# Splitting the merged rows where they are made, keeping the parts in DRAM for W_mix_out, and putting A11 and A12 together on TensorE

## The chip, the cores and the metric

The kernel runs on one core of one Trainium2 chip. The metric is the device time of one execution in microseconds (us). Three runs of the kernel before gave 2270.32, 2273.77 and 2274.34 us, so its median is 2273.77 us. The profile was taken of one further execution.

## The reference, cut to what matters

One layer works on 1024 tokens of width 1024. It is a half-step feed-forward layer, a token-mixing layer and a second half-step feed-forward layer, each between two RMS norms. All matrices are float32. The change lies at the end of the token mixing and at the start of the second feed-forward layer:

```python
def _token_mixing(u, ...):
    ...
    y_ret = (jax.nn.silu(rg) * y) @ w_ret_out
    y_na = _neighborhood_attention(...) @ w_na_out
    merged = jax.nn.sigmoid(g_ret) * y_ret + jax.nn.sigmoid(g_na) * y_na
    return merged @ w_out                      # W_mix_out, 1024 x 1024

    m = _token_mixing(_rms_norm(x, mix_pre_norm[l]), ...)
    x = x + _rms_norm(m, mix_post_norm[l])
    h = _swiglu(_rms_norm(x, ffn2_pre_norm[l]), ffn2_w_in[l], ffn2_w_out[l])
    x = x + 0.5 * _rms_norm(h, ffn2_post_norm[l])
```

## The kernel before, in words

**Float32 products out of three.** Every operand of a product is split into a high part in the type float32r (a cast on ScalarE, L60) and a low part, the rest (a subtraction on VectorE, L61); `Core.split` does both. `mm3` then multiplies high by high, high by low and low by high into one PSUM bank (L87, L88, L89). A product of two 128 x 128 and 128 x 512 blocks is therefore three matmuls, and each 128 x 512 operand costs one ScalarE and one VectorE instruction. `load_w` loads one 512 KB row block of a weight (issued by SyncE into a tile `wraw`, of which there are four) and splits it into two pieces `wh`, `wl`. There are nine places for each of `wh` and `wl`; a piece keeps its place until the last matmul that reads it.

**W_ret_out (L1295 to L1316).** The product is made transposed, one block of 128 features (a *row*) at a time, in groups of rows 0 to 2, 3 to 5, 6 and 7. A row has two banks of 512 tokens; six banks serve the products, so row 3 takes the banks of row 0. In the first group the loop over the eight blocks of the contraction is outside, so that all three rows end together; later rows come one after the other. VectorE reads a row's banks, multiplies them by the retention gate (L1314) and adds the other branch `z` (L1315); the merged row `m` then goes to DRAM (GpSimd issues that store, L67).

**W_mix_out (`out_proj`, L158).** Tokens are the rows of this product. Its groups are token tiles 0 to 2, 3 to 5, 6 and 7 (128 tokens each), and each group runs over all eight blocks k of the contraction. So each row block of W_mix_out and each merged row is fetched again in every group: for every k, `load_w` loads and splits W_mix_out's row block, and `lhs` in `stream` (L678) loads the merged row's columns of these tokens into `graw` and splits them into `gh`, `gl`. In the last three k of a group the loop over tokens is outside, so the tiles of a group end one after the other. Behind each tile comes `Ep`: squares on ScalarE (L219), the norm's factor on GpSimd (`rstd`, L97), scaling and residual on VectorE (L226, L228), a store of the new x issued by GpSimd (L67), squares and `rstd` again, and the second norm (L117). Some matmuls later TensorE transposes the tile (`flip`, L126) and `Winograd.put` files it.

**Winograd factors (`put`, L258).** The second feed-forward layer's first product is done with seven half-size products. For tokens 0 to 511 `put` splits the transposed tile into A11 and A12. For tokens 512 to 1023 it makes A22 and the four sums S1 to S4; S3 and S4 need A11 and A12 again, which are there only as parts, so VectorE subtracts from the high part (L275, L286) and adds the low part (L276, L287).

**Order.** `tc.tile_pool` hands out the buffers, and a scheduler fixes each engine's order when the program is built, ahead of the run. Each engine then works strictly in that order and waits at an instruction for the semaphores it names. Loads that SyncE issues are told by semaphores DMAHW0 to 7, transfers that GpSimd issues by DMASW0 to 7.

**Behind it (`Pairs.lead`, L346).** Twelve products with A11 and A12, "leads", run ahead of the second feed-forward layer and cover the last tiles' norms. Six results wait in PSUM or in the freed `gh`, `gl`, `graw` tiles (`save`).

## Time and profile before

| | |
|---|---|
| median of 3 runs | 2273.77 us |
| the profiled execution | 2273.08 us |
| its span, first to last instruction | 2271.3 us |
| TensorE matmul busy | 2211.0 us, 97% |
| VectorE busy | 1699.6 us, 75% |
| ScalarE busy | 1004.9 us, 44% |
| GpSimd busy | 577.1 us, 25% |
| mean granted TensorE clock | 0.993 |
| DMA | 424.72 MB, mean 187 GB/s |

A row of the profile names the line of the kernel, the engine, the operation and the tiles (out<-in). L60 and L61 are the two halves of a split wherever it is called from, so these rows are told apart by their tiles: `wl<-wraw,wh` belongs to a weight, `gl<-graw,gh` to the streamed rows. Times count from the first instruction. W_ret_out runs from about 1428 to 1516 us, W_mix_out's three groups from there to about 1624 us, and the leads until 1659 us. "POOL" is GpSimd, "SPq" the queue of SyncE. A DMA issued by GpSimd shows as a POOL instruction for the time of its issue; the transfer itself is told by its time to landing.

### The profile page before, as it was taken

What the parts mean: (1) busy time and instruction counts of PE and PEld (TensorE: products, weight loads), DVE (VectorE), ACT (ScalarE), POOL (GpSimd) and SP (SyncE); (2) the same over time, 40 slices, a digit from 0 to 9 for tenths busy, and PEclk for the clock granted to TensorE, in tenths of its full rate; (3) what the DMA queues carried; (4) which work ended last, traced back from release to release, by engine and by line L of the source; (5) the groups of instructions that cost most, each with busy time, mean ns of one, the idle gap of its engine ahead of it and who ended that gap; (6) DMA issues with size and microseconds to landing.
All of it is one profiled execution on the core that took longest, in us unless ns stands there. A gap on an engine that the chain in (4) does not pass through costs nothing.

```text
span 2271.3 us, 30229 instructions
## 1 busy us (share of the span) xinstructions
PE 2211.0 (97%) x10288; PEld 1837.1 (81%) x10288; DVE 1699.6 (75%) x2952; ACT 1004.9 (44%) x2117; POOL 577.1 (25%) x741
## 2 busy tenths in 40 slices
...
GB/s 192 105 170 184 186 183 186 165 271 199 236 176 144 149 194 111 135 196 245 206 163 170 163 218 228 296 211 213 177 114 188 195 189 176 185 139 237 198 234 151
DMA packets 162459, 424.72 MB, mean 187 GB/s; under 512 B 19776, under 2 KB 47552, under 8 KB 162240
## 3 DMA queue, kind: packets, MB, share of 16 engines
...
q14 instruction: 74, 0.61, 0.1%
...
## 4 chain that ended last, share of the span: by engine, by line
PE 42%; issue 7%; DVE 4%; DMA 3%; ACT 2%; POOL 1%; SPq 0%; POOLq 0%; DVEq 0%; ACTq 0%
PE ps L87 13%; PE ps L89 13%; PE ps L88 13%; DMA wraw<-in_dram 1%; PE pt L88 1%; PE pt L87 1%; PE pt L89 1%; DVE wl L61 1%; POOL rstd L97 1%; DMA vraw<-rv 0%; ACT wh L60 0%; DVE x L538 0%; DMA sn<-ev 0%; DVE tmp L117 0%; DMA vraw<-nvg 0%
## 5 line engine op out<-in xcount | busy, mean ns | idle before, releaser
L61 DVE TENSOR_TENSOR wl<-wraw,wh 128x512 fp32r<-128x512 f32 x662 | 479.8, 748 | 88.2 <-ACT wh L60 86.1
L60 ACT CAST wh<-wraw 128x512 fp32r<-128x512 f32 x670 | 390.6, 618 | 244.8 <-PE ps L88 71.0
L87 PE MATMUL ps<-wh,gh 128*128 128x512 f32 x612 | 239.7, 395 | 6.9 <-ACT gh L60 6.1
L88 PE MATMUL ps<-wl,gh 128*128 128x512 f32 x612 | 240.6, 394 | 0.7 <-DVE wl L61 0.7
L89 PE MATMUL ps<-wh,gl 128*128 128x512 f32 x612 | 235.2, 395 | 2.0 <-DVE gl L61 2.0
L61 DVE TENSOR_TENSOR gl<-graw,gh 128x512 fp32r<-128x512 f32 (+2 forms) x178 | 130.4, 736 | 141.0 <-ACT gh L60 138.1
L60 ACT CAST gh<-graw 128x512 fp32r<-128x512 f32 (+2 forms) x178 | 106.5, 601 | 197.8 <-PE ps L88 83.0
L87 PEld LDWEIGHTS ps<-wh,gh 128*128 128x128 f32 x612 | 116.3, 190 | 33.9 <-ACT gh L60 7.8
L89 PEld LDWEIGHTS ps<-wh,gl 128*128 128x128 f32 x612 | 116.1, 191 | 28.3 <-DVE gl L61 4.5
L528 POOL TENSOR_TENSOR q<-q,gain 128x512 f32<-128x512 f32 x30 | 52.8, 1779 | 335.7 <-ACT junk L527 124.0
L88 PEld LDWEIGHTS ps<-wl,gh 128*128 128x128 f32 x612 | 116.3, 190 | 25.2 <-DVE wl L61 1.5
L60 ACT CAST wh<-t 128x512 fp32r<-128x512 f32 x58 | 36.1, 622 | 214.9 <-DVE t L386 214.9
L87 PE MATMUL ps<-a11h,wh 128*128 128x512 f32 x280 | 110.6, 395 | 1.5 <-ACT wh L60 1.5
L87 PE MATMUL ps<-a12h,wh 128*128 128x512 f32 x280 | 110.8, 396 | 0.7 <-ACT wh L60 0.6
L87 PE MATMUL ps<-a22h,wh 128*128 128x512 f32 x280 | 109.8, 392 | 0.0
L89 PE MATMUL ps<-a22h,wl 128*128 128x512 f32 x280 | 109.1, 390 | 0.5 <-DVE wl L61 0.5
L89 PE MATMUL ps<-a12h,wl 128*128 128x512 f32 x280 | 109.6, 391 | 0.0
L88 PE MATMUL ps<-a11l,wh 128*128 128x512 f32 x280 | 109.6, 391 | 0.0
L89 PE MATMUL ps<-a11h,wl 128*128 128x512 f32 x280 | 109.6, 391 | 0.0
L88 PE MATMUL ps<-a12l,wh 128*128 128x512 f32 x280 | 109.4, 391 | 0.0
L88 PE MATMUL ps<-a22l,wh 128*128 128x512 f32 x280 | 109.1, 390 | 0.0
L97 POOL TENSOR_TENSOR rstd<-ss,mhalf 128x1 f32<-128x1 f32 x80 | 59.4, 745 | 184.6 <-DVE ss L221 74.4
...
## 6 DMA issues: line engine op xcount, KB each, us to landing
wraw<-in_dram SPq DMA_DIRECT2D x247, 512.0 KB, 4.4
lead<-in_dram POOLq DMA_DIRECT2D x44, 256.0 KB, 3.8
g0s<-cmb POOLq DMA_DIRECT2D x44, 256.0 KB, 3.0
graw<-g0s SPq DMA_DIRECT2D x44, 256.0 KB, 2.7
wq<-in_dram POOLq DMA_DIRECT2D x44, 256.0 KB, 4.0
g1s<-cmb POOLq DMA_DIRECT2D x44, 256.0 KB, 3.6
graw<-g1s SPq DMA_DIRECT2D x44, 256.0 KB, 2.7
...
```

The source lines that it names most:

```text
L60: nc.scalar.copy(h, src)
L61: (eng or nc.vector).tensor_tensor(l, src, hf, ALU.subtract)
L87: mm(ps, a[0], b[0], start=start, stop=False, skip_group_check=more)
L88: mm(ps, a[0], b[1], start=False, stop=False, skip_group_check=more)
L89: mm(ps, a[1], b[0], start=False, stop=stop, skip_group_check=more)
L97: self.nc.gpsimd.tensor_tensor(r[:, :n], ms, self.mhalf[:, :n], ALU.pow)
L528: (eng or c.nc.gpsimd).tensor_tensor(h if out is None else out, h, self.post[:, b * 512:(b + 1) * 512], ALU.mult)
```

## The change

Three things are done.

**1. Parts instead of rows.** `m` is split right after L1315 of the old kernel, in the W_ret_out loop, into tiles `mh` and `ml` (one buffer each), and both parts are stored to DRAM arrays (`mparts`), where one float32 row was stored. `stream` loads `gh` and `gl` from there, with two DMAs issued by GpSimd, where it loaded `graw` with one of SyncE's and split it. `graw` is gone; `gh` and `gl` have four buffers each instead of three, and the leads' six saved results are cut from these eight tiles.

**2. W_mix_out's blocks.** In the same loop, behind each row i, `load_w` loads and splits row block i of W_mix_out and four stores put its parts into DRAM (`wparts`). In W_mix_out itself the first two groups load and split as before (16 calls); the third group, tokens 768 to 1023, loads the parts: four DMAs of 256 KB issued by GpSimd for each k, no split.

**3. A11, A12.** With an identity matrix in float32r, TensorE adds the two parts of A11 (A12) into a PSUM bank of the tag `pt` (`less`), and VectorE does one subtraction from there instead of a subtraction and an addition. This is used in this stage alone (`whole` is called only for it).

In numbers of instructions, by the code: in the W_ret_out stage 16 more splits for `m`, 16 for W_mix_out, 8 more loads of 512 KB, 40 more stores (48 for 8). In the W_mix_out stage 24 splits fewer for the streamed rows and 16 fewer for the weights, 24 loads of SyncE replaced by 48 of GpSimd, 8 loads of 512 KB replaced by 32 of 256 KB, 8 VectorE additions fewer and 16 matmuls more.

```diff
@@ -242,7 +242,7 @@
     def __init__(self, c, pools, tmp, bufs, spill=None):
-        self.c, self.tmp, self.spill = c, tmp, spill
+        self.c, self.tmp, self.spill, self.ident = c, tmp, spill, None
         self.pools, self.bufs, self.ops = dict(zip(self.NAMES, (pools[i] for i in (0, 0, 1, 2, 2, 2, 2)))), bufs, {}
...
@@ -253,6 +253,23 @@
         return [q[:, :, ts] for q in self.op(n)]
+
+    def whole(self, pool):
+
+        self.ident = pool.tile([P, P], F32R, tag="identr", name="identr", bufs=1)
+        self.c.nc.scalar.copy(self.ident, self.c.ident)
+
+    def less(self, out, n, ts, b):
+
+        nc, (h, l) = self.c.nc, self.part(n, ts)
+        if self.ident is None:
+            nc.vector.tensor_tensor(out, h.bitcast(F32), b, ALU.subtract)
+            nc.vector.tensor_tensor(out, out, l.bitcast(F32), ALU.add)
+            return
+        bank = self.c.bank("pt", 2).rearrange("p (k t) -> p k t", k=4)
+        for j, p in enumerate((h, l)):
+            nc.tensor.matmul(bank, self.ident, p, start=j == 0, stop=j == 1)
+        nc.vector.tensor_tensor(out, bank, b, ALU.subtract)
     def put(self, t, g, pt):
...
@@ -264,16 +281,12 @@
             return self.tmp.tile([P, 4, P], F32, tag="cmb", name="cmb", bufs=4)
-        h1, l1 = [q.bitcast(F32) for q in self.part("a11", ts)]
-        h2, l2 = [q.bitcast(F32) for q in self.part("a12", ts)]
-
         if g == 0:
...
                 c.store(self.spill[:, :, ts], self.a21)
-            nc.vector.tensor_tensor(self.s3, h1, self.a21, ALU.subtract)
-            nc.vector.tensor_tensor(self.s3, self.s3, l1, ALU.add)
+            self.less(self.s3, "a11", ts, self.a21)
             return
...
@@ -283,8 +296,7 @@
         c.split(*self.part("s2", ts), s3)
-        nc.vector.tensor_tensor(s3, h2, s3, ALU.subtract)
-        nc.vector.tensor_tensor(s3, s3, l2, ALU.add)
+        self.less(s3, "a12", ts, s3)
         return lambda: c.split(*self.part("s4", ts), s3)
@@ -678,12 +690,10 @@
         p0 = toks[0] * P
-        raw = pool.tile([P, 384], F32, tag="graw", name="graw", bufs=2)
-        h = pool.tile([P, 384], F32R, tag="gh", name="gh", bufs=3)
-        l = pool.tile([P, 384], F32R, tag="gl", name="gl", bufs=3)
-        c.nc.sync.dma_start(raw[:, :n], src(k)[:, p0:p0 + n])
-        c.split(h[:, :n], l[:, :n], raw[:, :n])
-        return {t: (h[:, j * P:(j + 1) * P], l[:, j * P:(j + 1) * P]) for j, t in enumerate(toks)}
+        a = [pool.tile([P, 384], F32R, tag=g, name=g, bufs=4) for g in ("gh", "gl")]
+        for q, part in zip(a, src):
+            c.nc.gpsimd.dma_start(q[:, :n], part[k, :, p0:p0 + n])
+        return {t: [q[:, j * P:(j + 1) * P] for q in a] for j, t in enumerate(toks)}
     return lhs
@@ -1053,8 +1063,9 @@
         "rv": dt("rv", [TT, P, D]), "rg": dt("rg", [8, P, S]), "ry": dt("ry", [8, P, S]),
-        "sr": dt("sr", [8, P, S]), "sn": dt("sn", [8, P, S]), "z": dt("z", [8, P, S]), "m": dt("m", [8, P, S]),
+        "sr": dt("sr", [8, P, S]), "sn": dt("sn", [8, P, S]), "z": dt("z", [8, P, S]),
     }
+    mparts, wparts = ([dram.tile([KT, P, S], F32R, name=f"{n}{q}") for q in "hl"] for n in ("m", "wm"))
     def rows(a):
...
@@ -1313,7 +1324,15 @@
                 nc.vector.tensor_tensor(m[i][:, hs], m[i][:, hs], z[i][:, hs], ALU.add)
-            c.store(d["m"][i], m[i])
+            parts = [ro.tile([P, S], F32R, tag=f"m{q}", name=f"m{q}", bufs=1) for q in "hl"]
+            for h in range(2):
+                hs = slice(h * 512, (h + 1) * 512)
+                c.split(*[q[:, hs] for q in parts], m[i][:, hs])
+            for q, p in zip(mparts, parts):
+                c.store(q[i], p)
+            for h, a in enumerate(c.load_w(wmo[i])):
+                for q, p in zip(wparts, a):
+                    c.store(q[i][:, h * 512:(h + 1) * 512], p)
     y_stack.close()
...
@@ -1322,18 +1341,28 @@
     with tc.tile_pool(name="ep2", bufs=1) as ep:
-        rest = c.out_proj(KT, stream(c, gs, lambda k: d["m"][k]), lambda k: c.load_w(wmo[k]),
+        wx.whole(ep)
+        loads = []
+
+        def wload(k):
+            loads.append(k)
+            if len(loads) <= 2 * KT:
+                return c.load_w(wmo[k])
+            w = [[c.wpool.tile([P, 512], F32R, tag=g, name=g, bufs=9) for g in ("wh", "wl")] for _ in range(2)]
+            for h, a in enumerate(w):
+                for q, p in zip(wparts, a):
+                    nc.gpsimd.dma_start(p, q[k][:, h * 512:(h + 1) * 512])
+            return w
+        rest = c.out_proj(KT, stream(c, gs, mparts), wload,
                           Ep(c, ep, gmb, g2a, False, rows(x1), rows(x2), wx.put))
...
             if not places:
-                h, l, r = ([gs.tile([P, 384], F32, tag=n, name=n, bufs=b) for _ in range(b)]
-                           for n, b in (("gh", 3), ("gl", 3), ("graw", 2)))
-                for e in (h, l):
-                    places.extend([[e[0], e[1][:, :128]], [e[1][:, 128:], e[2][:, :256]]])
-                places.extend([[r[0], r[1][:, :128]], [r[1][:, 128:], h[2][:, 256:], l[2][:, 256:]]])
+                for n in ("gh", "gl"):
+                    e = [gs.tile([P, 384], F32, tag=n, name=n, bufs=4) for _ in range(4)]
+                    places.extend([[e[0], e[1][:, :128]], [e[1][:, 128:], e[2][:, :256]], [e[2][:, 256:], e[3]]])
             return places.pop(0)
...
```

The scheduler fixes the order anew. On every engine the order is the same as before up to W_ret_out; it differs from there to the leads. Three places are shown, as rows of an engine's order with the semaphores that each instruction waits for (PE, DVE, Activation and Pool are those of the engines).

**VectorE at the end of W_ret_out's rows 0 to 2.** Before (`wraw_14729`, `_14745`, `_14761` are W_ret_out's rows 3, 4 and 5; L1314 is the first reading of row 0's banks):

```order
L61 TENSOR_TENSOR wl_14732<-wraw_14729,wh_14731 128x512 [waits DMAHW7_49,Activation_49]
L61 TENSOR_TENSOR wl_14736<-wraw_14729,wh_14735 128x512 [waits Activation_49]
L61 TENSOR_TENSOR wl_14748<-wraw_14745,wh_14747 128x512 [waits DMAHW2_49,Activation_49]
L61 TENSOR_TENSOR wl_14752<-wraw_14745,wh_14751 128x512 [waits PE_49,Activation_49]
L61 TENSOR_TENSOR wl_14764<-wraw_14761,wh_14763 128x512 [waits DMAHW3_49,PE_49,Activation_49]
L61 TENSOR_TENSOR wl_14768<-wraw_14761,wh_14767 128x512 [waits PE_49,Activation_49]
L1314 TENSOR_TENSOR m_14554<-ps_14552,m_14554 128x512 [waits DMAHW5_49,PE_49]
L1314 TENSOR_TENSOR m_14554<-ps_14553,m_14554 128x512 [waits PE_49]
```

Now (`wraw_14729`, `_14755`, `_14781` are W_mix_out's blocks 0, 1 and 2, `_14795` and `_14811` are W_ret_out's rows 3 and 4; L1325 is the old L1314):

```order
L61 TENSOR_TENSOR wl_14732<-wraw_14729,wh_14731 128x512 [waits DMAHW7_49,Activation_49]
L61 TENSOR_TENSOR wl_14736<-wraw_14729,wh_14735 128x512 [waits Activation_49]
L61 TENSOR_TENSOR wl_14758<-wraw_14755,wh_14757 128x512 [waits DMAHW0_49,Activation_49]
L61 TENSOR_TENSOR wl_14762<-wraw_14755,wh_14761 128x512 [waits PE_49,Activation_49]
L61 TENSOR_TENSOR wl_14784<-wraw_14781,wh_14783 128x512 [waits DMAHW1_49,PE_49,Activation_49]
L61 TENSOR_TENSOR wl_14788<-wraw_14781,wh_14787 128x512 [waits PE_49,Activation_49]
L61 TENSOR_TENSOR wl_14798<-wraw_14795,wh_14797 128x512 [waits DMAHW2_49,DMASW6_49,Activation_49]
L61 TENSOR_TENSOR wl_14802<-wraw_14795,wh_14801 128x512 [waits DMASW0_49,Activation_49]
L61 TENSOR_TENSOR wl_14814<-wraw_14811,wh_14813 128x512 [waits DMAHW5_49,DMASW2_49,Activation_49]
L61 TENSOR_TENSOR wl_14818<-wraw_14811,wh_14817 128x512 [waits DMASW4_49,Activation_49]
L1325 TENSOR_TENSOR m_14557<-ps_14555,m_14557 128x512 [waits PE_49]
L1325 TENSOR_TENSOR m_14557<-ps_14556,m_14557 128x512 [waits PE_49]
```

Ten splits of weights stand ahead of the first reading of row 0 where there were six. The last four wait, beside ScalarE, for DMASW6, 0, 2 and 4: these are the landings of the stores of the low pieces of W_mix_out's blocks 0 and 1, whose places `wl` the pieces of rows 3 and 4 take.

**GpSimd in W_mix_out's third group** (tokens 768 to 1023), while the epilogues of the second group's tiles run. Before (`epx_15726`, `epx_15767` and `epx_15808` are token tiles 3, 4 and 5):

```order
L97 TENSOR_TENSOR rstd_15732<-ss3_15728,mhalf_74 128x1 [waits DVE_49,Pool_49]
L67 DMA x2_101<-epx_15726 128x1024 [waits DMAHW6_49,DMASW0_49,DVE_49]
L97 TENSOR_TENSOR rstd_15744<-ss3_15734,mhalf_74 128x1 [waits DVE_49,Pool_49]
L97 TENSOR_TENSOR rstd_15773<-ss3_15769,mhalf_74 128x1 [waits DVE_49,Pool_49]
L67 DMA x2_101<-epx_15767 128x1024 [waits DMAHW0_49,DMASW1_49,DVE_49]
L97 TENSOR_TENSOR rstd_15785<-ss3_15775,mhalf_74 128x1 [waits DVE_49,Pool_49]
L97 TENSOR_TENSOR rstd_15814<-ss3_15810,mhalf_74 128x1 [waits DVE_49,Pool_49]
L67 DMA x2_101<-epx_15808 128x1024 [waits DMAHW5_49,DMASW2_49,DVE_49]
L97 TENSOR_TENSOR rstd_15826<-ss3_15816,mhalf_74 128x1 [waits DVE_49,Pool_49]
```

Now, from the first norm of token tile 5 (`epx_15949`) on; the `wh`, `wl`, `gh`, `gl` ahead of L67 are those of block k = 3, the ones behind it those of k = 4:

```order
L97 TENSOR_TENSOR rstd_15955<-ss3_15951,mhalf_74 128x1 [waits DVE_49,Pool_49]
L1354 DMA wl_16101<-wml_119 128x512 [waits DMASW5_49]
L1354 DMA wh_16102<-wmh_118 128x512 [waits DMASW6_49,PE_49,Activation_49]
L1354 DMA wl_16103<-wml_119 128x512 [waits DMASW7_49]
L695 DMA gh_16108<-mh_116 128x256 [waits DMASW0_49,PE_49]
L695 DMA gl_16109<-ml_117 128x256 [waits DMASW1_49,PE_49]
L67 DMA x2_101<-epx_15949 128x1024 [waits DMAHW1_49,DMASW2_49,DVE_49]
L97 TENSOR_TENSOR rstd_15967<-ss3_15957,mhalf_74 128x1 [waits DVE_49,Pool_49]
L1354 DMA wh_16128<-wmh_118 128x512 [waits DMASW3_49,Activation_49]
L1354 DMA wl_16129<-wml_119 128x512 [waits DMASW4_49]
L1354 DMA wh_16130<-wmh_118 128x512 [waits DMASW5_49,PE_49]
L1354 DMA wl_16131<-wml_119 128x512 [waits DMASW6_49]
```

The issues of the third group's loads stand between the norms and the stores of the epilogues. Those of k = 4 come behind token tile 5's store, which waits for VectorE, and behind its second norm factor.

**VectorE for the factors of token tile 4.** Before (L275/L276 and L286/L287 are the sums with A11 and A12, `wl` and `gl` the low parts of W_mix_out's pieces and of streamed rows):

```order
L281 TENSOR_TENSOR cmb_15931<-pt_15936,cmb_15931 128x512
L61 TENSOR_TENSOR s3l_15947<-cmb_15932,s3h_15946 128x4x128 [waits Activation_49]
L61 TENSOR_TENSOR wl_15974<-wraw_15967,wh_15973 128x512
L283 TENSOR_TENSOR cmb_15932<-pt_15936,cmb_15932 128x512 [waits DVE_49]
L61 TENSOR_TENSOR s1l_15952<-cmb_15931,s1h_15951 128x4x128 [waits Activation_49]
L61 TENSOR_TENSOR gl_15979<-graw_15977,gh_15978 128x256 [waits DMAHW7_49]
L61 TENSOR_TENSOR s2l_15956<-cmb_15932,s2h_15955 128x4x128 [waits Activation_49]
L61 TENSOR_TENSOR wl_16002<-wraw_15999,wh_16001 128x512 [waits DMAHW3_49]
L286 TENSOR_TENSOR cmb_15932<-a12h_15485,cmb_15932 128x512 [waits DVE_49]
L61 TENSOR_TENSOR wl_16006<-wraw_15999,wh_16005 128x512
L287 TENSOR_TENSOR cmb_15932<-cmb_15932,a12l_15486 128x512 [waits DVE_49]
L61 TENSOR_TENSOR gl_16011<-graw_16009,gh_16010 128x256 [waits DMAHW2_49]
```

Now (L272 is the subtraction in `less`, from a bank `pt` that TensorE fills; the old L283 is L296):

```order
L294 TENSOR_TENSOR cmb_16060<-pt_16067,cmb_16060 128x512 [waits DVE_49]
L117 SCALAR_TENSOR_TENSOR tmp_15965<-epx_15949,rstd_15967,gpre_15261 128x512 [waits Pool_49]
L117 SCALAR_TENSOR_TENSOR tmp_15965<-epx_15949,rstd_15967,gpre_15261 128x512
L61 TENSOR_TENSOR s3l_16078<-cmb_16061,s3h_16077 128x4x128 [waits Activation_49]
L61 TENSOR_TENSOR s1l_16083<-cmb_16060,s1h_16082 128x4x128 [waits Activation_49]
L296 TENSOR_TENSOR cmb_16061<-pt_16067,cmb_16061 128x512 [waits DVE_49]
L61 TENSOR_TENSOR s2l_16087<-cmb_16061,s2h_16086 128x4x128 [waits Activation_49]
L272 TENSOR_TENSOR cmb_16061<-pt_16090,cmb_16061 128x512 [waits DVE_49,PE_49]
```

The two instructions each for A11 and A12 are one each, which wait for TensorE, and no splits of weights or of streamed rows stand in between.

## The prediction

> **What bounds the kernel now.** I read the page first, for what carries the whole, and then the change's stage in windows.
>
> ```profile
> PE 2211.0 (97%) x10288; PEld 1837.1 (81%) x10288; DVE 1699.6 (75%) x2952; ACT 1004.9 (44%) x2117; POOL 577.1 (25%) x741
> ```
>
> ```profile
> PE ps L87 13%; PE ps L89 13%; PE ps L88 13%; DMA wraw<-in_dram 1%; PE pt L88 1%; PE pt L87 1%; PE pt L89 1%; DVE wl L61 1%; POOL rstd L97 1%; DMA vraw<-rv 0%; ACT wh L60 0%; DVE x L538 0%; DMA sn<-ev 0%; DVE tmp L117 0%; DMA vraw<-nvg 0%
> ```
>
> TensorE bounds the program, and the chain that ended last is its products; so only TensorE's gaps and its clock can be won or lost. The change touches a stage of 231 us, which has to be read by itself. The windows are W_ret_out's rows 0 to 2, its rows 3 to 7, W_mix_out's three groups and the leads; behind the span stand the engines' busy times, the granted clock, the DMA share and GB/s:
>
> ```profile
> core 0: us, PE busy (x) PEld busy (x) DVE busy (x) ACT busy (x) POOL busy (x), PEclk, DMA share, GB/s
> 1428.70:1460.80 32.10, 32.10 (x142) 26.57 (x143) 16.16 (x20) 11.69 (x15) 0.96 (x2) 1.00 0.91 339
> 1460.80:1515.90 55.10, 55.10 (x245) 45.63 (x244) 24.63 (x41) 7.61 (x14) 3.78 (x7) 1.00 0.64 218
> 1515.90:1549.70 33.80, 33.80 (x151) 27.94 (x149) 17.73 (x32) 15.15 (x35) 3.01 (x5) 1.00 0.63 214
> 1549.70:1586.40 36.70, 36.08 (x170) 29.16 (x168) 30.06 (x55) 23.00 (x55) 5.63 (x10) 1.00 0.71 240
> 1586.40:1623.90 37.50, 30.71 (x120) 22.70 (x119) 33.96 (x61) 22.62 (x51) 3.65 (x6) 0.86 0.56 175
> 1623.90:1659.30 35.40, 34.09 (x158) 27.68 (x157) 32.47 (x55) 22.80 (x52) 6.29 (x10) 1.00 0.47 153
> ```
>
> TensorE is full up to group 2. In group 3 VectorE is busy for 33.96 of 37.50 us, TensorE idles for 6.8 us and runs at clock 0.86. How much is lost there: a matmul of 512 columns follows the last in 0.227 us, as these starts show:
>
> ```profile
> 1460.57 0.39 PE L89 MATMUL ps<-xy,wl 128*128 128x512 f32 x1
> 1460.80 0.39 PE L87 MATMUL ps<-xy,wh 128*128 128x512 f32 x1
> ```
>
> Group 3 has two tiles, two banks, eight k and three products, 96 matmuls or 21.8 us, and 24 transposes, for which I estimate half a matmul each (2.7 us): 24.5 us. So 13 us are lost, and group 3 is where the change can win. What fills VectorE there, by groups of instructions (count, busy us, mean ns):
>
> ```profile
> L61 DVE TENSOR_TENSOR wl<-wraw,wh 128x512 fp32r<-128x512 f32 x15 | 9.9, 689 | 0.0
> L61 DVE TENSOR_TENSOR gl<-graw,gh 128x256 fp32r<-128x256 f32 x6 | 2.5, 422 | 0.0
> L287 DVE TENSOR_TENSOR cmb<-cmb,a12l 128x512 f32<-128x512 f32 x2 | 1.4, 690 | 0.0
> L276 DVE TENSOR_TENSOR cmb<-cmb,a11l 128x512 f32<-128x512 f32 x2 | 1.4, 684 | 0.0
> ```
>
> In W_ret_out it is the DMA that is full. Before row 3 starts, at 1460.80 us:
>
> ```profile
> 1440.00:1445.00 5.00, 5.00 (x24) 4.14 (x23) 3.28 (x3) 2.11 (x2) 0.00 (x0) 1.00 1.01 391
> 1445.00:1450.00 5.00, 5.00 (x24) 4.14 (x23) 0.25 (x1) 0.90 (x2) 0.00 (x0) 1.00 1.03 420
> 1450.00:1455.00 5.00, 5.00 (x24) 4.14 (x23) 2.54 (x5) 2.24 (x5) 0.00 (x0) 1.00 1.03 415
> 1455.00:1460.00 5.00, 5.00 (x24) 4.14 (x23) 2.82 (x5) 0.91 (x2) 0.00 (x0) 1.00 0.71 262
> ```
>
> So about 410 GB/s is all that the queues moved together.
>
> **W_ret_out, term one: +8 us.** Added are 8 loads of 512 KB, 32 stores of 256 KB and 8 of 512 KB: 16.8 MB. Before, the two windows moved 339 x 32.1 + 218 x 55.1 = 22.9 MB. The sum of 39.7 MB takes 97 us at 410 GB/s, where the two windows have 87.2. Not all of it must be over by then: the last three rows' parts (3.1 MB) are stored behind W_mix_out's first loads, and some 1.5 MB are loads ahead for later k. By bytes alone, with the DMA full throughout, the stage changes by -2 to +10 us; in the first window it was at 0.91, 3 us short, which makes it +1 to +13.
>
> The order tells where TensorE would feel it. VectorE's rows, in time:
>
> ```profile
> 1453.44 2.65 DVE L61 TENSOR_TENSOR wl<-wraw,wh 128x512 fp32r<-128x512 f32 x4 [2.40 <-ACT wh L60]
> 1458.28 1.37 DVE L1314 TENSOR_TENSOR m<-ps,m 128x512 f32<-128x512 f32 x2 [2.18 <-PE ps L89]
> ```
>
> Before, the last weight of the six was split at 1456.1, and VectorE waited 2.2 us for row 0's banks. It freed them with 1.1 us to spare: row 3 takes them at 1460.80. Now ten splits stand ahead of that reading, and the last four also wait for the landing of the stores of W_mix_out's blocks 0 and 1. Behind them on VectorE are the readings of rows 0, 1 and 2, so TensorE stops at row 3. Block 0 can be split no sooner than `wl` at 1449.75 did it for row 3, whose place in SyncE's queue it takes; its store joins a full DMA. What landings cost there:
>
> ```profile
> wraw<-in_dram SPq DMA_DIRECT2D x2, 512.0 KB, 10.2
> ...
> wraw<-in_dram SPq DMA_DIRECT2D x1, 512.0 KB, 7.0
> m<-m POOLq DMA_DIRECT2D x1, 512.0 KB, 8.0
> ```
>
> The first are loads issued from 1441 to 1444; the others are a load and a store, both issued at 1474.7. The loads of rows 3 and 4 and the stores of blocks 0 and 1, with block 1's and 2's loads ahead of them, are 1.5 MB loads and 2.1 MB stores, of which about 2.5 MB are more than stood there before: 6.1 us at 410 GB/s. Counted from 1456.1 the last split ends at 1462.2, the two L1314 (1.37 us) at 1463.6: 2.8 us late if the two queues share evenly. If the store's queue gets only a third of the rate, 2.1 MB take 15.3 us from 1449.8, to 1465.1, and with two splits and the reading to 1467.9: 7.1 us late. Below it is zero, if block 1's stores land within 8 us. I take 5.
>
> A wait of that length also costs clock. Elsewhere in the program:
>
> ```profile
> 1009.88 0.45 PE L746 MATMUL ps<-k,qh 128*128 128x384 f32 x1 [3.92 <-DVE nast L747]
> ...
> 1010.00:1015.00 5.00, 2.84 (x8) 1.79 (x8) 2.92 (x8) 4.10 (x9) 1.26 (x1) 0.56 0.89 317
> 1015.00:1020.00 5.00, 3.82 (x12) 3.24 (x13) 4.78 (x12) 4.95 (x14) 1.35 (x1) 0.50 1.01 357
> 1020.00:1025.00 5.00, 5.00 (x30) 4.51 (x29) 4.43 (x13) 3.91 (x10) 1.62 (x3) 0.91 0.91 287
> ```
>
> After one wait of 3.92 us the clock is at 0.5 to 0.56 for about 10 us, a loss of up to 5.1 us with TensorE full. I take 3, since half of the stall may come in pieces: 5 + 3 = 8, inside the bytes' +1 to +13. Range 0 to 12.2. The Trainium skill ("TensorE: Matmul & The Clock Gate", section on HAM oscillation) says that idle gaps over about 3.4 us throttle the array again. The trace agrees with 3.92 us; by that rule a stall of 2.8 us would lose no clock, and the term would be 2.8 instead of 8. Against the rule stands this, in group 3 (the waits' columns are total, times, longest):
>
> ```profile
> PE pt L126 <- DVE tmp L117: 2.3, 1, 2.3
> ...
> 1600.00:1605.00 5.00, 3.74 (x12) 2.37 (x13) 5.00 (x10) 2.23 (x4) 0.00 (x0) 0.61 0.50 125
> ```
>
> There the longest single wait was 2.3 us and the clock fell to 0.61.
>
> The 16 + 16 splits of the stage cost VectorE 32 x 0.69 = 22 us and ScalarE as much, where VectorE has 16.16 + 24.63 of 87.2 us busy: hidden. The 40 more issues of GpSimd, at 0.57 us from the row below, are 23 us beside 4.7 busy: hidden too.
>
> **W_mix_out's groups 1 and 2: +0.5 us** (-2 to +4). VectorE loses 16 splits of streamed rows, about 10 us, which it doesn't lack in group 1 and hardly in group 2 (TensorE idles for 0.62 us). Against that, the first `gl` stands on GpSimd behind all stores of blocks 0 to 7, 44 transfers from the first on. If the backlog of the bytes above is not gone by then, group 1 starts late; that time is the upper end, since what W_ret_out has lost by then isn't lost again.
>
> **Group 3, term two: -6 us.** 12 splits of weights and 6 to 8 of streamed rows go, and four additions: 9.9 + 2.5 + 1.4 + 1.4 = 15.2 us of VectorE's 33.96 are gone, and 18.8 left are no bound in 24.5. What is late next is GpSimd. Its rows before, with T0 = 1586.40 the group's start:
>
> ```profile
> 1593.76 0.59 POOL L97 TENSOR_TENSOR rstd<-ss,mhalf 128x1 f32<-128x1 f32 x1 [2.32 <-DVE ss L221]
> 1597.29 0.57 POOL L67 DMA_DIRECT2D x<-epx  x1 [2.95 <-DVE epx L228]
> 1598.46 0.87 POOL L97 TENSOR_TENSOR rstd<-ss,mhalf 128x1 f32<-128x1 f32 x1 [0.60 <-DVE ss L113]
> ...
> 1640.94 2.34 POOL L478 DMA_DIRECT2D wq<-in_dram  x4 [3.51 <-DVE cmb L275]
> wq<-in_dram POOLq DMA_DIRECT2D x4, 256.0 KB, 3.9
> ```
>
> Four issues take 2.34 us, 0.585 each, and land 3.9 us later. GpSimd now issues 48 in this group, 28 us. The 24 of k = 4 to 7 stand behind token tile 5's store and second factor, which ended at T0 + 12.9; with VectorE freer I estimate T0 + 11.6. Then 23 issues bring k = 7's `gh` to T0 + 25.1, its landing to about T0 + 28.5 (it is half of 256 KB), and the 12 matmuls of k = 7 follow: 2.7 us, T0 + 31.2. Against 37.5 that is -6.3; I take -6, for a wait or a lower clock in the last k. Bounds: -9.5 (TensorE needs its 24.5 us, 1.8 for tiles 4 and 5's eight matmuls in `less`, 0.227 each, and half a landing) and -3 (it runs at half clock from T0 + 28). 5.2 MB in 14 us are 370 GB/s, just below what the DMA can do.
>
> **Leads: +2.5 us** (+1 to +3). Eight of the 16 matmuls in `less`, those of tiles 6 and 7, fall here, at 0.227 us: 1.8. The order on TensorE mixes the two tiles' last matmuls, so the tiles end nearer to each other, and the second's transposes wait longer for an epilogue that GpSimd's rows from 1593.76 on show to take some 5 us; I estimate 2 us, in place of the 1.3 us that TensorE idled here before (35.40 - 34.09). 1.8 + 2 - 1.3 = 2.5. The sum on the profiled 2273.08 us: 8 + 0.5 - 6 + 2.5 = 5, 2278.1; the median lies 0.7 above that execution: **2279 us**, slower by 0.2%.
>
> **The rivals.** *Faster: the transfers are in time.* The stores of blocks 0 and 1 land as the `wq` did, in 3.9 us, so no split waits and row 3 starts on time (0), and in group 3 the landings keep up too (-9.5). Then 2273.8 + 0.5 - 9.5 + 2.5 = 2267 us. For it: the DMA falls to 0.71 from 1455 on, and row 3 alone is needed at once. Against it: 1.01 to 1.03 up to then, and the bytes. It decides if block 1's last store lands before about 1458.
>
> *Slower: the store queue gets a third.* The stall is 7.1 us and the clock loses its full 5.1: 12.2 instead of 8, 2283 us. For it: the store of 8.0 us was slower than the load of 7.0 beside it. Against it: not by much, which is nearer to even. It decides if that landing comes after 1463. The Trainium skill ("DMA: Bandwidth & Descriptors", section on queues, rings and completion order) says that each engine goes round the queues that have work, packet by packet. By that, two queues share evenly, and the stall is 2.8 us, 2279 - 5 = 2274 with no clock lost, inside the own range given below; 8.0 against 7.0 us agrees roughly.
>
> *Slower: group 3 is not shortened.* Loads that wait for places, for the epilogue on GpSimd and for each other (each waits for the eighth before it) take VectorE's place, and the group still takes 37 us: 2279 + 6 = 2285 us. Against it: 13 us are lost now, and VectorE's share of them really goes.
>
> **How the numbers follow.** Chances: forecast 0.42, transfers in time 0.23, a third 0.22, group 3 as long as now 0.13. What a measurement of this kernel tells from no change is about 0.2%, 4.5 us: 2269.2 to 2278.3. The forecast's own range is 2271 to 2286 (W_ret_out's 8 by -5 or +3, group 3 by -3.5 or +3); of its chance 0.02 lies below, 0.18 within, 0.22 above. The first rival gives 0.21 to faster and 0.02 to the same, the second 0.20 to slower and 0.02 to the same, the third 0.13 to slower. Faster 0.23, same 0.22, slower 0.55. The range of 2266 to 2288 leaves out the far ends of the rivals.
>
> **What would show it.** Right: in the profile after, TensorE waits at row 3 of W_ret_out for VectorE, the last `wl` ahead of L1325 ends after 1459 and was released by a store's landing, the clock dips behind it, and the DMA is near 1.0 for most of the stage; group 3's window shows VectorE near 19 us, GpSimd near 28 and a length of some 31 us, its idle time put down to parts from DRAM. Wrong: TensorE full through row 3 (then the first rival), group 3's parts all there before they are needed or, the other way, a group of 37 us; or a wait that I priced at nothing, at the first k of W_mix_out above all.

## The result and the profile after

| | before | changed |
|---|---|---|
| median | 2273.50 us (4 runs, 2270.32 to 2274.34) | 2298.55 us (4 runs, 2297.27 to 2302.32) |
| ratio | 1 | 1.0117, 95% interval 1.0105 to 1.0130 |
| span of the profiled execution | 2271.3 us | 2295.5 us |

The change made the kernel 25 us slower. The sign is the one forecast, the time lies outside the range of 2266 to 2288.

Stages are compared from the first matmul of one to the first of the next. Row 3's first matmul before was at 1461.47 us and group 3's at 1585.25 us; the prediction's window bounds, 1460.80 and 1586.40, were up to 1.2 us off, which moves none of its terms by more than that. All lengths below are so taken, in us.

| kernel | rows 0 to 2 and the wait for row 3 | rows 3 to 7 | group 1 | group 2 | group 3 | leads | sum |
|---|---|---|---|---|---|---|---|
| before | 32.77 | 54.41 | 32.64 | 36.73 | 38.69 | 35.34 | 230.58 |
| changed | 39.03 | 56.28 | 45.62 | 38.60 | 38.72 | 36.75 | 255.00 |
| difference | +6.26 | +1.87 | +12.98 | +1.87 | +0.03 | +1.41 | +24.42 |
| predicted | +8 for this and the next | | +0.5 for this and the next | | -6 | +2.5 | +5 |

The stage holds the whole loss. (W_ret_out starts 2.7 us later in the changed kernel's profile, from differences ahead of the change, and behind the leads some 2.9 us come back.) The windows of the changed kernel, in the columns of the prediction's windows:

```profile
1431.39:1470.42 39.03, 33.22 (x144) 26.90 (x145) 17.26 (x21) 13.52 (x18) 7.09 (x13) 0.95 1.03 365
1470.42:1526.70 56.28, 56.17 (x240) 46.08 (x241) 30.41 (x50) 16.23 (x30) 19.57 (x38) 0.97 1.07 361
1526.70:1572.32 45.62, 37.51 (x145) 29.55 (x145) 26.01 (x44) 17.95 (x38) 12.70 (x24) 0.89 0.89 298
1572.32:1610.92 38.60, 36.98 (x170) 29.04 (x168) 23.66 (x42) 16.04 (x40) 17.04 (x31) 1.00 0.93 298
1610.92:1649.64 38.72, 32.00 (x134) 23.44 (x133) 25.63 (x42) 16.57 (x36) 22.97 (x44) 0.96 1.08 316
1649.64:1686.39 36.75, 35.79 (x164) 28.90 (x163) 28.05 (x48) 22.27 (x51) 6.21 (x10) 1.00 0.41 143
```

The DMA, at 0.56 to 0.91 of its time before, is now full or nearly so in every stage up to the leads. VectorE's load in group 3 fell from 34.67 us (the row of before in the corrected bounds follows) to 25.63, by 9.0 us where 15.2 were forecast, and the group is as long as it was.

```profile
1585.25:1623.94 38.69, 31.91 (x126) 23.64 (x125) 34.67 (x64) 23.81 (x53) 4.28 (x7) 0.87 0.57 181
```

Where TensorE stopped (its timeline, the cause in brackets):

```profile
1470.42 0.77 PE L87 MATMUL ps<-xy,wh 128*128 128x512 f32 x1 [5.76 <-ACT wh L60]
...
1527.89 0.50 PE L89 MATMUL ps<-wh,gl 128*128 128x512 f32 x1 [0.48 <-DMA gl<-ml]
1532.06 0.80 PE L87 MATMUL ps<-wh,gh 128*128 128x512 f32 x1 [2.97 <-DVE m L1325]
1539.64 0.79 PE L87 MATMUL ps<-wh,gh 128*128 128x512 f32 x1 [4.65 <-DVE m L1325]
```

The first is row 3, where the prediction had put it. The others stand in W_mix_out's first group, and two of them wait for L1325: VectorE had not yet read W_ret_out's last rows, whose banks the group takes. VectorE at the first place:

```profile
1452.43 3.81 DVE L61 TENSOR_TENSOR wl<-wraw,wh 128x512 fp32r<-128x512 f32 x6 [4.88 <-ACT wh L60]
1462.22 0.69 DVE L61 TENSOR_TENSOR wl<-wraw,wh 128x512 fp32r<-128x512 f32 x1 [5.98 <-issue]
1465.78 0.69 DVE L61 TENSOR_TENSOR wl<-wraw,wh 128x512 fp32r<-128x512 f32 x1 [2.87 <-DMA wml<-wl]
1467.27 0.69 DVE L61 TENSOR_TENSOR wl<-wraw,wh 128x512 fp32r<-128x512 f32 x1 [0.79 <-ACT wh L60]
1468.98 0.69 DVE L61 TENSOR_TENSOR wl<-wraw,wh 128x512 fp32r<-128x512 f32 x1 [1.03 <-DMA wml<-wl]
1469.60 1.28 DVE L1325 TENSOR_TENSOR m<-ps,m 128x512 f32<-128x512 f32 x2
```

The ten splits ahead of L1325 are as the order showed them: six of W_mix_out's blocks, then four of rows 3 and 4, two of them released by `DMA wml<-wl`, the landing of a store. L1325 began at 1469.60, where it began at 1458.28 before (2.7 us of this lie ahead of the stage).

The profile puts the end of TensorE's wait at row 3 down to a cast of `wh` by ScalarE that began at 1469.76 and took 0.62 us. That cast is the fifth behind those of W_mix_out's first blocks, and the four before it belong to rows 3 and 4, so row 3 doesn't need it. What row 3 still lacked was its bank: the first L1325 began at 1469.60 and took some 0.7 us. In the kernel without the merged row's parts (an experiment below, where the line is L1327) the profile names that reading for the same stop:

```profile
1469.94 0.77 PE L87 MATMUL ps<-xy,wh 128*128 128x512 f32 x1 [5.57 <-DVE m L1327]
```

At the second place the same happens with the later rows:

```profile
1507.10 1.28 DVE L1325 TENSOR_TENSOR m<-ps,m 128x512 f32<-128x512 f32 x2
...
1515.82 1.29 DVE L61 TENSOR_TENSOR ml<-m,mh 128x512 fp32r<-128x512 f32 x2 [5.64 <-ACT mh L60]
...
1524.71 1.29 DVE L61 TENSOR_TENSOR wl<-wraw,wh 128x512 fp32r<-128x512 f32 x2 [3.97 <-DMA wml<-wl]
1525.92 1.28 DVE L1325 TENSOR_TENSOR m<-ps,m 128x512 f32<-128x512 f32 x2
...
1531.33 1.28 DVE L1325 TENSOR_TENSOR m<-ps,m 128x512 f32<-128x512 f32 x2
...
1537.09 1.29 DVE L61 TENSOR_TENSOR ml<-m,mh 128x512 fp32r<-128x512 f32 x2 [2.68 <-DMA ml<-ml]
...
1538.90 1.28 DVE L1325 TENSOR_TENSOR m<-ps,m 128x512 f32<-128x512 f32 x2
```

The last three L1325 are rows 5, 6 and 7. W_ret_out's products ended at 1526.4, and a row takes TensorE 10.9 us, so row 5's banks were complete at about 1505; VectorE read them 21 us later. In between it split and waited. Its waits for stores from 1461 to 1540 (total, times, longest), and the landings of the stores that it waited for (KB each, median us):

```profile
DVE ml L61 <- DMA ml<-ml: 10.6, 4, 3.9
DVE wl L61 <- DMA wml<-wl: 9.1, 4, 4.0
...
ml<-ml POOLq DMA_DIRECT2D x7, 512.0 KB, 6.5
wmh<-wh POOLq DMA_DIRECT2D x12, 256.0 KB, 7.8
wml<-wl POOLq DMA_DIRECT2D x12, 256.0 KB, 7.7
```

The longest stop of group 1, 4.65 us, can be followed back in the trace: GpSimd issued the store of one row's `ml` at 1530.50, it landed 6.5 us later, the next row's `ml` began at 1537.09, the last L1325 stood behind it at 1538.90, and TensorE went on at 1539.64.

In group 3 GpSimd's queue, and behind it TensorE:

```profile
1623.13 0.54 POOL L67 DMA_DIRECT2D x<-epx  x1
1626.56 0.56 POOL L97 TENSOR_TENSOR rstd<-ss,mhalf 128x1 f32<-128x1 f32 x1 [2.90 <-DVE ss L113]
1627.09 0.57 POOL L1354 DMA_DIRECT2D wh<-wmh  x1
...
1642.25 0.57 POOL L1354 DMA_DIRECT2D wl<-wml  x1
...
1648.59 0.50 PE L88 MATMUL ps<-wl,gh 128*128 128x512 f32 x1 [0.24 <-DMA wl<-wml]
```

The loads of k = 4 to 7 begin behind token tile 5's second factor, 16.2 us into the group, the last is issued at 31.3 and is used at 37.7, just as the group ends.

### The profile page after: what moved, and what is told of

The parts are those of the page before. It is cut to its first block, busy times and chain, and to the rows that moved or that the text cites. A ratio compares the mean times of both kernels' runs of the same rounds, so it can differ in the third digit from the quotient of the medians.

```text
span 2295.5 us, 30417 instructions
## 1 busy us (share of the span) xinstructions
PE 2221.4 (97%) x10304; PEld 1842.5 (80%) x10304; DVE 1695.7 (74%) x2935; ACT 1004.4 (44%) x2109; POOL 638.9 (28%) x861
## 4 chain that ended last, share of the span: by engine, by line
PE 39%; issue 9%; DMA 5%; POOL 3%; DVE 2%; ACT 1%; SPq 0%; POOLq 0%; DVEq 0%; ACTq 0%
PE ps L89 12%; PE ps L87 12%; PE ps L88 12%; DMA wml<-wl 1%; DMA gl<-ml 1%; PE pt L87 1%; PE pt L88 1%; PE pt L89 1%; DMA ml<-ml 1%; POOL rstd L97 1%; PE pt L775 0%; DMA wraw<-in_dram 0%; PE ps L756 0%; DVE wl L61 0%; DVE x L550 0%
## 5 line engine op out<-in xcount | busy, mean ns | idle before, releaser
L61 DVE TENSOR_TENSOR gl<-graw,gh 128x512 fp32r<-128x512 f32 x154 | 116.8, 762 | 131.7 <-ACT gh L60 128.7
L60 ACT CAST gh<-graw 128x512 fp32r<-128x512 f32 x154 | 95.3, 621 | 182.5 <-PE ps L88 78.8
L414 DVE TENSOR_TENSOR c<-ps,gt 128x512 f32<-128x512 f32 x44 | 30.4, 690 | 91.2 <-PE ps L89 90.9
```

What stands on the lines that cost most here:

```text
L60: nc.scalar.copy(h, src)
L61: (eng or nc.vector).tensor_tensor(l, src, hf, ALU.subtract)
L414: self.last = self.read = tt(c21, p7, c12, ALU.add).ins
```

## The experiments

The theories: 1, the two losses around W_ret_out come from W_mix_out's splits, which stand on VectorE ahead of the readings of banks and wait for stores; 2, they come from the bytes alone; 3, they come from the single buffers of the merged row's parts. For group 3: GpSimd's order, or the transfers. Ratios are to the kernel before, timed on the same chip; the table of stages is of each kernel's profiled execution, as differences from the stages before ("wait for row 3" is the stage of rows 0 to 2 with that wait).

| kernel | median us | ratio (95%) | wait for row 3 | rows 3 to 7 | group 1 | group 2 | group 3 | leads |
|---|---|---|---|---|---|---|---|---|
| m's parts and sums by TensorE | 2267.81 | 0.9979 (0.9970 to 0.9989) | 0.0 | 0.0 | 0.0 | +1.0 | -8.4 | +2.0 |
| sums by TensorE alone | 2270.87 | 0.9991 (0.9982 to 1.0000) | +0.9 | 0.0 | 0.0 | 0.0 | -4.7 | +2.1 |
| m's parts alone | 2271.87 | 0.9996 (0.9987 to 1.0006) | 0.0 | 0.0 | 0.0 | +1.2 | -3.1 | 0.0 |
| without m's parts | 2286.66 | 1.0059 (1.0042 to 1.0076) | +6.1 | +1.4 | +2.0 | +1.7 | -2.6 | +5.0 |
| two buffers for m's parts | 2294.40 | 1.0083 (1.0066 to 1.0100) | +6.1 | +1.8 | +10.4 | +1.0 | +1.8 | +1.6 |
| before, with more stores | 2283.50 | 1.0039 (1.0026 to 1.0052) | 0.0 | 0.0 | +9.7 | +0.3 | +0.4 | 0.0 |
| one z for all rows | 2290.54 | 1.0081 (1.0066 to 1.0096) | +6.1 | +1.5 | +6.9 | +1.1 | +0.1 | +1.4 |
| blocks split by GpSimd | 2303.24 | 1.0135 (1.0118 to 1.0153) | +1.6 | +0.1 | +24.7 | +1.5 | +3.6 | +1.6 |
| parts of k = 4 to 7 alone | 2275.64 | 1.0017 (1.0007 to 1.0027) | 0.0 | 0.0 | +8.1 | +0.9 | -8.5 | +1.5 |
| parts stored in groups 1 and 2 | 2296.73 | 1.0084 (1.0057 to 1.0112) | +0.5 | 0.0 | +4.3 | +11.6 | -2.0 | +1.6 |
| group 3's loads by SyncE | 2292.19 | 1.0080 (1.0063 to 1.0098) | +6.5 | +3.5 | +13.2 | +0.8 | -4.3 | +1.1 |
| the first, sums for tiles 4, 5 | 2266.38 | 0.9978 (0.9968 to 0.9988) | 0.0 | 0.0 | 0.0 | +0.9 | -8.7 | +0.8 |

**Without W_mix_out's parts.**

```diff
-            for h, a in enumerate(c.load_w(wmo[i])):
-                for q, p in zip(wparts, a):
-                    c.store(q[i][:, h * 512:(h + 1) * 512], p)
...
-        rest = c.out_proj(KT, stream(c, gs, mparts), wload,
+        rest = c.out_proj(KT, stream(c, gs, mparts), lambda k: c.load_w(wmo[k]),
```

> The changed kernel without W_mix_out's blocks in W_ret_out: nothing of W_mix_out is loaded, split or stored there, and the third token group loads and splits its blocks like the first two. The merged rows are still split and stored as parts. Theory 1 (the 8 us in W_ret_out and the 13 us in W_mix_out's first group come from W_mix_out's splits, which stand on VectorE ahead of the readings of banks and wait for stores to free their places): both losses go, group 3 keeps the splits of streamed rows and the additions saved: 2267 to 2273 us. Theory 2 (the bytes themselves, of which a quarter, 4.2 of 16.8 MB, stays): a quarter of 21 us stays, 2276 to 2280. Theory 3 (the single buffers of the two parts of m, whose splits wait for the row before to land): most of the 13 us of group 1 stays, 2283 or more.

2267.81 us, 5.5 us faster than before and in theory 1's interval. Both losses around W_ret_out are gone and group 3 is 8.4 us shorter, so W_mix_out's blocks in W_ret_out, with their loads, splits and stores, are necessary for the losses and unnecessary for the gain. Group 3 and the leads of this kernel:

```profile
1587.53:1617.80 30.27, 28.36 (x133) 21.96 (x131) 27.45 (x47) 19.33 (x42) 9.59 (x17) 1.00 0.85 250
1617.80:1655.10 37.30, 36.45 (x165) 29.11 (x165) 32.35 (x56) 24.38 (x55) 6.51 (x10) 1.00 0.50 169
```

VectorE still splits all weights in that group and is busy for 27.45 of 30.27 us, and TensorE idles for 1.9 us at full clock. Of the forecast's 15.2 us less of VectorE work, the part that came from the weights was not needed.

**The sums alone.** The kernel before, with `less` and `whole` and nothing else:

```diff
+        wx.whole(ep)
         rest = c.out_proj(KT, stream(c, gs, lambda k: d["m"][k]), lambda k: c.load_w(wmo[k]),
```

> The kernel before with nothing changed but A11 and A12 put together by TensorE. If VectorE bounds group 3, the four additions that go there (2.8 us of the 34.67 it is busy) show as 1 to 3 us: 2271 to 2273. If the matmuls and the wait of VectorE for TensorE cost as much as they save: 2273 to 2276. Nothing here can give more than 3 us either way.

2270.87 us, on the edge of what can be told. Group 3 is 4.7 us shorter, more than the 2.8 us of VectorE work taken away and more than the 3 us that the expectation held possible in all; 2.1 us go back in the leads. The granted clock in group 3 rose from 0.87 to 0.95 (the row below): fewer waits also slowed TensorE less.

```profile
1585.67:1619.64 33.97, 30.47 (x133) 23.23 (x132) 32.25 (x60) 22.96 (x52) 3.97 (x7) 0.95 0.60 196
```

**The merged row's parts alone**, that is the first experiment without the sums:

```diff
-        wx.whole(ep)
```

> The merged rows split and stored as parts, nothing else: W_mix_out's blocks loaded and split in every group as before, A11 and A12 put together by VectorE as before. With the sums by TensorE as well the kernel took 2267.8, group 3 8.4 us shorter; the sums alone made group 3 4.7 us shorter and the leads 2.1 longer. If the two add up: group 3 is 3 to 4 us shorter, the leads unchanged, 2269 to 2272. If either alone frees VectorE enough: group 3 6 to 8 us shorter, 2265 to 2268.

2271.87 us, the first case, and no difference from before that can be told; group 3 is 3.1 us shorter in the profiled execution, which with 2275.15 us took longer than the median. 4.7 and 3.1 add up to 7.8, near the 8.4 of both together.

**W_mix_out's parts without the merged row's.** The sums by TensorE stay:

```diff
-            parts = [ro.tile([P, S], F32R, tag=f"m{q}", name=f"m{q}", bufs=1) for q in "hl"]
-            for h in range(2):
-                hs = slice(h * 512, (h + 1) * 512)
-                c.split(*[q[:, hs] for q in parts], m[i][:, hs])
-            for q, p in zip(mparts, parts):
-                c.store(q[i], p)
+            c.store(d["m"][i], m[i])
```

> The changed kernel with the merged rows as before: one float32 row each in DRAM, loaded by SyncE and split in W_mix_out. W_mix_out's blocks are loaded, split and stored in W_ret_out, and group 3 loads their parts through GpSimd. Theory 1: W_ret_out loses 6 to 9 us and W_mix_out's first group 8 to 13, as in the changed kernel: 2290 to 2300. Theory 2 (12.6 of the 16.8 MB stay): three quarters of 21 us, 2287 to 2292. Theory 3: the first group's 13 us are gone, the 6 us at row 3 stay: 2280 to 2285.

2286.66 us, below theory 1's interval, just under theory 2's and above theory 3's. The wait for row 3 stands (+6.1), the first group's loss is down to 2.0. So the first wait needs W_mix_out's blocks alone, the second needs them and the merged row's parts. Theory 1 as stated is wrong for the second. (Without the parts 4.2 MB of stores are missing as well, so this run doesn't tell the splits of the merged row from their bytes.) The leads' 5.0 us are a wait of 2.1 us for a norm and a clock of 0.96; they weren't followed up.

**Two buffers for each part of the merged row.**

```diff
-            parts = [ro.tile([P, S], F32R, tag=f"m{q}", name=f"m{q}", bufs=1) for q in "hl"]
+            parts = [ro.tile([P, S], F32R, tag=f"m{q}", name=f"m{q}", bufs=2) for q in "hl"]
```

> The changed kernel with two buffers instead of one for each part of a merged row. Theory 1 (W_mix_out's splits): the waits of ml for the store before it (10.6 us in four waits on VectorE) go to the splits of W_mix_out behind them, 0 to -3 us: 2295 to 2299. Theory 3 (the single buffers): W_mix_out's first group gets back 6 to 12 us, 2286 to 2292.

2294.40 us, 0.6 us below theory 1's interval and 2.4 above theory 3's; group 1 loses 10.4 instead of 13.0. VectorE's waits for stores between 1470 and 1545 (total, times, longest) mostly change hands; in the changed kernel they were 5.2 us for `wml` and 12.3 for `ml`:

```profile
DVE wl L61 <- DMA wml<-wl: 15.4, 5, 6.3
...
DVE ml L61 <- DMA ml<-ml: 4.5, 1, 4.5
```

Theory 3 alone is out.

**More stores and no splits.** The kernel before, each merged row stored four more times, twice whole and twice in halves:

```diff
             c.store(d["m"][i], m[i])
+            c.store(extra[0][i], m[i])
+            for j in range(4):
+                hs = slice(j % 2 * 512, (j % 2 + 1) * 512)
+                c.store(extra[1 + j // 2][i][:, hs], m[i][:, hs])
+            c.store(extra[3][i], m[i])
```

> The kernel before with 16.8 MB of further stores in W_ret_out, which nobody needs: behind each row its merged row is stored again twice whole and twice in two halves, 2.1 MB more per row, all issued by GpSimd, with no split and no further load. Theory 2 (the bytes alone): most of the loss of the changed kernel's W_ret_out and first group (21 us) appears, 2285 or more. Theory 1 (what is queued on VectorE and ScalarE behind the landings): the loads come later, but no engine's order has a wait for these stores ahead of a reading of banks; 0 to 6 us, 2273 to 2280.

2283.50 us, between both. W_ret_out's rows 3 to 7:

```profile
1461.42:1515.82 54.40, 54.40 (x242) 45.05 (x240) 23.60 (x39) 7.16 (x14) 22.58 (x42) 1.00 1.02 401
```

They take 54.40 us as before, at a DMA share of 1.02 and 401 GB/s: a full DMA by itself stops nothing there. (These stores begin behind row 0, so they say nothing on the wait for row 3.) The loss comes in group 1 and in another way than in the changed kernel:

```profile
1533.72 0.51 ACT L60 CAST gh<-graw 128x384 fp32r<-128x384 f32 x1 [5.52 <-DMA graw<-m]
...
1540.25 0.51 ACT L60 CAST gh<-graw 128x384 fp32r<-128x384 f32 x1 [4.98 <-DMA graw<-m]
```

ScalarE waits for the rows themselves, whose stores queue behind the others on GpSimd; no row here waits for L1316, the reading of the banks in this kernel. So a backlog of some MB on GpSimd's queue can cost the first group 9.7 us, three quarters of what the change costs it, but in another way than the changed kernel's trace shows.

**Fewer bytes, the same splits and stores.** One load of z for all rows:

```diff
             for q, name, src in ((m, "m", "sr"), (z, "z", "z")):
+                if name == "z" and i > 0:
+                    q[i] = z0
+                    continue
...
+            z0 = z[0] if i == 0 else z0
```

> The changed kernel without the loads of z for rows 1 to 7: row 0's z is added to every row (that part of the computation is left out). All splits, stores and the waits for them stay; 3.7 MB fewer are moved in W_ret_out, 36.0 instead of 39.7 MB. Theory 2b (bytes cost nothing up to what the DMA carries in the stage, 87.2 us x 410 GB/s = 35.8 MB, and all of the rest beyond it; the kernel with parts of W_mix_out alone had 35.5 MB and lost 2 us in the first group): the first group's 13 us shrink to 2 to 5, 2284 to 2291. Theory 1 (the order of the splits on VectorE and the latency of each store, whatever the rate): 9 to 13 us stay, 2293 to 2299.

2290.54 us, in theory 2b's interval, but group 1 loses 6.9 us, between the two: with 3.7 of 39.7 MB less, half of the loss is gone. The stores that VectorE waits for land a little sooner (medians of 7.1 us for `wml` and 6.2 for `ml`, from 7.7 and 6.5). But the order changed as well: the scheduler moved one more block ahead of row 3's reading, and VectorE's waits for stores from 1461 to 1540 add up to 25.7 us, not to fewer than the 19.7 of the changed kernel. So this run points at the bytes but doesn't show their share.

**W_mix_out's blocks split by GpSimd**, in buffers of their own:

```diff
-            for h, a in enumerate(c.load_w(wmo[i])):
-                for q, p in zip(wparts, a):
-                    c.store(q[i][:, h * 512:(h + 1) * 512], p)
+            raw = ro.tile([P, D], F32, tag="vraw", name="vraw", bufs=1)
+            nc.sync.dma_start(raw, wmo[i])
+            for h in range(2):
+                a = [ro.tile([P, 512], F32R, tag=g, name=g, bufs=2) for g in ("vh", "vl")]
+                s = raw[:, h * 512:(h + 1) * 512]
+                nc.gpsimd.tensor_copy(a[0], s)
+                nc.gpsimd.tensor_tensor(a[1], s, a[0].bitcast(F32), ALU.subtract)
+                for q, p in zip(wparts, a):
+                    c.store(q[i][:, h * 512:(h + 1) * 512], p)
```

> The changed kernel with W_mix_out's blocks in W_ret_out cast and split by GpSimd, in buffers of their own; the bytes, the stores and group 3 are as in the changed kernel, but nothing of these blocks stands on VectorE or ScalarE, and W_ret_out's pieces no longer wait for their places. Theory 1: row 3 starts within 1 us of its time and the first group loses 0 to 4 us: 2274 to 2282. Theory 2b: the same 3.9 MB are too many, the first group loses 8 to 13 us through later loads, and row 3 waits for its weights: 2286 to 2299.

2303.24 us, outside both intervals. TensorE's waits:

```profile
1463.47 0.47 PE L87 MATMUL ps<-xy,wh 128*128 128x512 f32 x1 [0.42 <-DVE m L1325]
...
1527.65 0.80 PE L87 MATMUL ps<-wh,gh 128*128 128x512 f32 x1 [6.78 <-DVE m L1325]
1557.24 0.76 PE L87 MATMUL ps<-wh,gh 128*128 128x512 f32 x1 [12.98 <-DMA gh<-mh]
```

With the same bytes the wait for row 3 is 0.42 instead of 5.76 us: the first loss came from W_mix_out's pieces on VectorE and ScalarE, their splits ahead of the reading and their stores, which held the places of the next pieces. (The run takes both away at once.) In group 1 the queue only moved: GpSimd now has the splits between the merged row's stores, the parts of the last rows are late by 13 us, and VectorE's `ml` still wait for those stores (26.1 us in six waits from 1463 to 1560). For group 1 this run can't separate bytes from order.

**Parts of W_mix_out for k = 4 to 7 alone**, made behind rows 3 to 6 and loaded in group 3 by SyncE:

```diff
-            for h, a in enumerate(c.load_w(wmo[i])):
-                for q, p in zip(wparts, a):
-                    c.store(q[i][:, h * 512:(h + 1) * 512], p)
+            if 3 <= i < 7:
+                for h, a in enumerate(c.load_w(wmo[i + 1])):
+                    for q, p in zip(wparts, a):
+                        c.store(q[i + 1][:, h * 512:(h + 1) * 512], p)
...
-            if len(loads) <= 2 * KT:
+            if len(loads) <= 2 * KT or k < 4:
...
-                    nc.gpsimd.dma_start(p, q[k][:, h * 512:(h + 1) * 512])
+                    nc.sync.dma_start(p.bitcast(F32), q[k][:, h * 512:(h + 1) * 512].bitcast(F32))
```

> The merged rows as parts, the sums by TensorE, and parts of W_mix_out for k = 4 to 7 alone, made behind rows 3 to 6 of W_ret_out and loaded in group 3 by SyncE; k = 0 to 3 are loaded and split in every group. W_ret_out moves 33.4 MB, below the 35.8 the DMA can carry, and row 3 has nothing new ahead of it. Theory 2b: W_ret_out and the first group lose 0 to 2 us, group 3 gains up to 3 us on the 30.3 that it takes without any parts of W_mix_out: 2264 to 2269. Theory 1: the splits behind rows 3 to 6 still hold the readings of rows 5 to 7, 4 to 8 us in the first group: 2271 to 2276.

2275.64 us, as theory 1 had it. Here the bytes are less than the DMA can carry by the estimate, and group 1 loses 8.1 us, so that limit is no threshold below which nothing is lost. The row of TensorE, and then VectorE's and GpSimd's, that lead up to it:

```profile
1525.00 0.80 PE L87 MATMUL ps<-wh,gh 128*128 128x512 f32 x1 [5.16 <-DVE m L1325]
...
1511.61 0.69 DVE L61 TENSOR_TENSOR wl<-wraw,wh 128x512 fp32r<-128x512 f32 x1 [3.77 <-DMA wml<-wl]
...
1516.80 0.54 POOL L67 DMA_DIRECT2D ml<-ml  x1 [0.61 <-DVE ml L61]
...
1517.02 1.28 DVE L1325 TENSOR_TENSOR m<-ps,m 128x512 f32<-128x512 f32 x2
...
1522.44 1.29 DVE L61 TENSOR_TENSOR ml<-m,mh 128x512 fp32r<-128x512 f32 x2 [2.34 <-DMA ml<-ml]
...
1524.26 1.28 DVE L1325 TENSOR_TENSOR m<-ps,m 128x512 f32<-128x512 f32 x2
```

This is the mechanism in one place. The store of one row's `ml` is issued at 1516.80 and lands some 5.5 us later; the next row's `ml` waits for it; and the reading of the last row, L1325, stands behind that `ml` in VectorE's order. The last row, whose products ended at about 1517, is read 7.2 us after the one before (1517.02 to 1524.26). When VectorE is in time such a step fits into TensorE's 10.9 us per row: in the first experiment VectorE waited 1.46 us for the last row's product. Here a weight's split had waited 3.77 us, until 1511.61, for the store of a piece of W_mix_out; such waits make VectorE late, and the last rows then come one behind the other. Group 3 took 30.22 us, against 30.27 without any of W_mix_out's parts: there was nothing for them to win.

**W_mix_out's parts stored where they are made anyway**, blocks 0 to 3 in group 1 and 4 to 7 in group 2:

```diff
             if len(loads) <= 2 * KT:
-                return c.load_w(wmo[k])
+                w = c.load_w(wmo[k])
+                if (k < KT // 2) == (len(loads) <= KT):
+                    for h, a in enumerate(w):
+                        for q, p in zip(wparts, a):
+                            c.store(q[k][:, h * 512:(h + 1) * 512], p)
+                return w
```

> The changed kernel with W_mix_out's parts stored where its blocks are split anyway: blocks 0 to 3 in the first token group, 4 to 7 in the second, by the same 32 stores; W_ret_out loads and splits nothing of W_mix_out. Group 3 loads the parts through GpSimd. Theory 1: W_ret_out and the start of the first group are as in the kernel before; in groups 1 and 2 the places of wh and wl come free some 6 us later, which costs 0 to 6 us, and group 3 takes 38 us again: 2273 to 2281. Theory 2 (bytes): groups 1 and 2 lose 5 to 10 us each: 2284 or more.

2296.73 us. The profiled execution took 2285.03 us, the other three 2296.18 to 2298.36, so the stages account for that one alone. Row 3 starts 0.5 us late, and W_ret_out is otherwise as before. Groups 1 and 2 lose 4.3 and 11.6 us; 9.2 of these are idle time, 7.6 of it in three waits for `gh<-mh`, and the rest is a lower clock (0.95 and 0.89). The streamed rows' loads stand behind the stores on GpSimd. Theory 1's interval missed the time and theory 2's held it, though not with 5 to 10 us in each group.

**Group 3's loads issued by SyncE.**

```diff
-                    nc.gpsimd.dma_start(p, q[k][:, h * 512:(h + 1) * 512])
+                    nc.sync.dma_start(p.bitcast(F32), q[k][:, h * 512:(h + 1) * 512].bitcast(F32))
...
-            c.nc.gpsimd.dma_start(q[:, :n], part[k, :, p0:p0 + n])
+            (c.nc.sync if len(toks) < 3 else c.nc.gpsimd).dma_start(q[:, :n].bitcast(F32), part[k, :, p0:p0 + n].bitcast(F32))
```

> The changed kernel with the 48 loads of parts in group 3 issued by SyncE instead of GpSimd; the same bytes in the same pieces. If GpSimd's strict order bounds group 3 (the loads of k = 4 to 7 stand behind token tile 5's second norm factor): group 3 takes 29 to 33 us instead of 38.7, 2290 to 2294 in all. If the transfers themselves bound it (256 KB and 128 KB pieces, DMA share 1.08 over the group at 316 GB/s): no change, 2297 to 2300.

2292.19 us. Group 3 takes 34.44 instead of 38.72 us, less gain than the 29 to 33 expected:

```profile
1609.74:1644.18 34.44, 30.46 (x133) 24.14 (x132) 25.03 (x41) 16.18 (x36) 3.20 (x6) 0.90 0.97 334
...
PE ps L87 <- DMA gh<-mh: 3.8, 1, 3.8
```

So taking these loads out of GpSimd's order is worth 4.3 us. (They also go through another queue here, as float32 instead of float32r, but they land hardly sooner: 256 KB after 5.3 and 5.5 us in the median, from 5.6 and 5.7.) One wait of 3.8 us for a transfer, and the lower clock, are left, at a DMA share of 0.97. The kernel without these loads does the group in 30.3.

**A faster one.** The first experiment, with the sums by TensorE for token tiles 4 and 5 alone:

```diff
-        if self.ident is None:
+        if self.ident is None or ts.start >= 2 * P:
```

> The merged rows as parts and nothing of W_mix_out in W_ret_out, as in the fastest kernel so far (2267.8), with the sums by TensorE for token tiles 4 and 5 alone; tiles 6 and 7, whose factors are made during the leads, take VectorE's two instructions again. If the leads' 2.0 us are the eight matmuls that the sums put there (1.8 us), they go and group 3 keeps its 8.4: 2265 to 2267. If VectorE is needed there (32 of 37 us busy), the leads lose as much in waits: 2267 to 2270.

2266.38 us, 0.9978 of before (0.9968 to 0.9988). The leads lose 0.8 instead of 2.0 us and group 3 keeps its gain, as the first case had it. The medians of this kernel and of the first experiment lie 1.4 us apart, too near to tell them apart; both beat the kernel before and the changed one.

## Why the prediction was right or wrong

**W_ret_out, +8: right**, 6.26 + 1.87 = 8.13 us. The wait for row 3 was 5.76 us for the 5 taken, in the place named and with the splits of rows 3 and 4 released by stores. That W_mix_out's pieces on VectorE and ScalarE made it is shown: without them there, and with the same bytes, it was 0.42 us. The clock cost less than the 3 us taken: TensorE's matmuls stood 0.43 us apart until 1473.55, and 0.23 from there, so 3.1 us at half clock cost about 1.5. That the sum came so near is in part luck: a longer stall, a smaller loss of clock and some 0.8 us that are neither add up to it.

**"The 16 + 16 splits ... hidden": the step that failed.** It compared busy times (22 us against some 46 free), and VectorE was indeed free for 25.9 of the 56.28 us of rows 3 to 7. But a split that waits for a store holds everything behind it while VectorE counts as idle. The prediction followed this at row 3 and stopped there; the same waits for stores (19.7 us for `ml` and `wl` from 1461 on) made the readings of rows 5 to 7 late, and the price came in W_mix_out's first group, where it had **+0.5** (with group 2, up to +4) and 14.85 were measured. Its last sentence names this place, the first k of W_mix_out, as a wait that it had priced at nothing. The remark that what W_ret_out has lost isn't lost again was wrong as well: TensorE's stop at row 3 gave VectorE no lead. Of group 1's 12.98 us, 8.1 are idle time and 4.9 a lower clock.

What makes it up is shown in part. W_mix_out's blocks in W_ret_out, their loads, splits and stores together, are necessary (0.0 without them), the merged row's parts nearly so (2.0 without them), two buffers take away 2.6, and one load of z for eight takes away 6.1. The traces fit a reading in which the order says who waits and the landings say how long, but that is argued and not shown. How the 13 us divide stays open: the one run that moved the splits moved them into GpSimd's queue, and none gave the pieces `wh` and `wl` more places.

**Group 3, -6: wrong**, 0.03. The mechanism was the one named, GpSimd's strict order, with each term too small: the second factor of tile 5 was over 16.2 us into the group instead of 11.6, the 24 issues took from there to 31.9 (15.7 us instead of 14, with 2.2 us of waits for the landings of earlier loads in it), and the last landing came 6.3 us behind its issue instead of 3.4. That is the third rival's case, which had 0.13. SyncE's queue takes 4.3 us of it away. The 3.9 us from the trace was the landing of 256 KB beside little else (`wq`, at 1641 us; the DMA share was 0.62 from 1641 to 1646 and 0.07 in the 5 us after), and the group ran at a share of 1.08; the prediction had itself worked out 370 GB/s for it, "just below what the DMA can do".

**VectorE's 15.2 us in group 3** were too many, and they were not the price. The 9.9 us in the sum are those of 15 splits, and the 12 that it names would be 8.3. In the changed kernel seven splits of weights are left in the group, which belong to the leads, and VectorE's time fell by 9.0 us:

```profile
L61 DVE TENSOR_TENSOR wl<-wraw,wh 128x512 fp32r<-128x512 f32 x7 | 4.4, 686 | 3.3 <-ACT wh L60 3.3
```

As to the price, the group became 4.7 us shorter without the four additions, 3.1 without the streamed rows' splits, and no shorter without half of W_mix_out's splits: it takes 30.2 us with seven splits of weights in it and 30.3 with thirteen.

**Leads, +2.5:** 1.41; 2.0 to 2.1 in the kernels with the sums and without W_mix_out's parts. That the eight matmuls make it is supported: without them it was 0.0 (the merged row's parts alone) and 0.8.

**The rivals.** Slower by a third of the rate had 2283 us by a longer stall at row 3; the stall was as forecast, so this isn't what happened. The range ended at 2288 because each rival changed one term; a group 1 that lost 13 us was in none of them.
